# Expert blocks of an MoE layer on one core: another order of the weight loads, another interleaving of large and small experts, and a shorter gather for the first small expert

## The chip, the cores and the metric

The kernel runs on one core of a Trainium2 chip. The metric is the device time of one execution in microseconds (us). A core has several engines with their own instruction streams, each worked off strictly in order: PE (TensorE, matrix products), DVE (VectorE), ACT (ScalarE), POOL (GpSimd) and SP (SyncE), which here issues nearly all transfers from memory (HBM) into the on-chip memory (SBUF). Results of PE land in PSUM, of which the other engines read them. An instruction that needs something of another engine waits for a semaphore, and everything behind it on its own engine waits too.

## The reference, cut to what matters

Two transformer blocks on 256 tokens of width 1024. Everything ahead of the last stage is left as it is; the change lies in the last stage, a mixture of eight experts, with two experts for each token:

```
def moe_swiglu(x, router_w, w_gate, w_up, w_down):
    logits = (x @ router_w).astype(jnp.float32)
    top_v, top_i = lax.top_k(logits, TOP_K)
    gates = jax.nn.softmax(top_v, axis=-1)
    combine = jnp.sum(jax.nn.one_hot(top_i, N_EXPERTS, dtype=jnp.float32) * gates[..., None], axis=-2)
    y = jnp.zeros_like(x)
    for e in range(N_EXPERTS):
        y = y + combine[..., e:e + 1].astype(x.dtype) * swiglu(x, w_gate[e], w_up[e], w_down[e])
    return y
```

`swiglu` is `(silu(x @ w_gate) * (x @ w_up)) @ w_down`, with 3584 hidden columns for each expert, all in float32. The three matrices of an expert are 44 MB, those of all eight 352 MB (336 loads of 1 MB), and each is read once.

## The kernel before

**Experts and blocks.** The experts are sorted by how many tokens they have and put into eight places, in turn a large and a small one. A place has a fixed number of token slots (`SLOTS`): 128 for the large ones (even places, called many here), 64, 64, 64 and 32 for the small ones (odd places, called few). The hidden columns of an expert are taken in 7 blocks of 512, so that there are 28 many blocks, m0 to m27, and 28 few blocks, f0 to f27. A block takes 6 loads of 1 MB: two halves each of gate, up and down.

**A many block.** Each half of weights goes through `weights`: a 1 MB load into a raw buffer, a rounded copy `whi` by ACT (L437, CAST), and the rest, weight minus `whi`, by DVE (L438), both for products in a faster number format, with three products for each tile: token-hi by weight-hi, token-lo by weight-hi, token-hi by weight-lo. `proj` does gate, then up; `act` makes silu(gate) times up (ACT L1919, DVE L1920); `turn` transposes it on PE into the PSUM tile `t`, from which ACT takes the rounded copy `mh` (L1940 CAST) and DVE the rest (L1940); `down` multiplies with the down weights, into the PSUM tiles `s`. Where a few block follows, the down weights of a many block are loaded and split ahead of that block's products and kept in `WD`.

**A few block.** The weights are multiplied straight from the raw buffers, in float32, without ACT and DVE (`passing`, `proj_few`). Gate and up stand side by side in one PSUM tile `mm`; after both halves `act` copies it to SBUF by ACT (`msg<-mm`, L1917 COPY), and `turn` transposes it and makes the product (L1934, L1935).

**The order.** The program is written block by block, and each engine gets its instructions in an order that follows from the code order and from priorities (`ahead` moves a piece forward). Inside block n stand: the first half of its products, `turn` of block n-1, the second half, `act`, then `down` of block n-1. So PE does the down products of a many block right behind the second half of the few block that follows it. The order of the blocks follows from `BEHIND`, by how many blocks the few ones lag: m0 m1 m2 f0 m3 f1 m4 f2 ... m27 f25 f26 f27.

**Buffers.** The raw buffers (called `room`, `raw`, and by the names of dead tiles: `x`, `xlo`, `oht`, `my`) are handed out in a ring in the order of the calls. SP issues a load only when its buffer has been read by its last user, and the loads behind it on SP wait as well.

**Gather.** `gather(q)` collects the tokens of place q and of place q+1 by products with a 0/1 matrix `oh`, from the hi and the lo part of the tokens apart. For the first few expert it is called a second time with `some=False`: 32 products of 256 columns, of which only the 64 slots of place 1 are taken over, by 8 DVE instructions (L1805, L1806).

Of the kernel before, what the change touches and what calls it, by code (L numbers as in the profile page):

```python
# [11 lines left out]
F32 = mybir.dt.float32  # L12
# [10 lines left out]
KC = 8  # L23
# [10 lines left out]
RANKS = (None, 3, 0, 4, 1, 5, 2, 6)  # L34
SLOTS = (128, 64, 128, 64, 128, 64, 128, 32)

BEHIND = 2.5, 2.5

SPLITS = (("dsa_q", 256), ("dsa_k", 64), ("dsa_v", 64), ("idx_q", 256), ("idx_k", 32), ("idx_w", 8),
          ("fox_q", 384), ("fox_k", 384), ("fox_v", 384), ("fox_f", 6), ("nsa_q", 384), ("nsa_kc", 128),  # L40
# [243 lines left out]
class Net:  # L284
# [1410 lines left out]
    def _moe(self, x, out):  # L1695
        nc, d, hw, tc = self.nc, self.d, self.hw, self.tc
        y = self.xp.tile([128, 2, D], F32, name="y", tag="xhi")
# [4 lines left out]
        oh = own("oh").rearrange("p (b e s) -> p b e s", b=2, e=NE)  # L1702
        rt = self.router.rearrange("p (k e) -> p k e", k=KC)
        bf = self.c["before"].rearrange("p (a b) -> p a b", a=8)
        at = self.psum("t")
        hold, kept = self.hold, []
        for tb in range(2):
            ts = slice(tb * 128, tb * 128 + 128)
            with self.ahead(5000):

                p = self.psum("o")
                for k in range(KC):
                    r = nc.tensor.matmul(p[:, 0:8], x[:, k, ts], rt[:, k], start=k == 0, stop=k == KC - 1)
                q = lg[:, tb]
# [17 lines left out]
                b = nc.vector.tensor_scalar(oh[:, tb, 0], self.c["iota"], slot[:, tb, 0:1], None, op0=ALU.is_equal)  # L1732

                for c in range(2):
                    p = self.psum("s" if tb else "mm")
# [4 lines left out]
                    i = self.split(xh[:, tb, cs], xl[:, tb, cs], p)  # L1740
                    if tb:
                        self.after(i, b)
                        b = i
# [19 lines left out]
        def back(oh, dt):  # L1763

            ohf = oh.bitcast(F32) if dt is F32R else oh
            oht = self.late.tile([128, NE, T], dt, name="oht", tag="oht")
            for e in range(0, NE, 2):
                p = self.psum()
                for i in range(2):
                    for tb in range(2):  # L1770
                        t = self.tr(p[:, i * 256 + tb * 128:i * 256 + tb * 128 + 128], ohf[:, tb, e + i], self.ident)
                        self.after(t, gm)
                i = nc.scalar.copy(oht[:, e:e + 2], p.rearrange("p (e t) -> p e t", e=2))
                self.after(i, gx)
            return oht

        own_g = own("g")
        gh, gl = (own_g[:, i * 1024:i * 1024 + 1024].rearrange("p (k s) -> p k s", k=KC) for i in range(2))

        FX = {}  # L1780

        def gather(q, tags="mm", low=nc.vector.tensor_copy, some=True, few=True):

            if few:
                w = SLOTS[q + 1]
                fx = FX[q + 1] = hw.tile([128, KC, 64], F32, name="fx", tag="fx", bufs=2)
            for k in range(0, KC, 2):
                for src, dst, ev, tag in ((xh, gh, nc.scalar.copy, tags), (xl, gl, low, tags)):
                    p = self.psum(tag)
                    for i in range(2):  # L1790
                        for tb in range(2):
                            o = oh[:, tb, q:q + 2] if few else oh[:, tb, q][:, None].to_broadcast([128, 2, 128])
                            last = self.mm(p[:, i * 256:i * 256 + 256], src[:, tb, (k + i) * 128:(k + i) * 128 + 128], o,
                                           start=tb == 0, stop=tb == 1)
                    p = p.rearrange("p (k s) -> p k s", k=2)
                    if src is xh:
                        ph = p
                        if some:
                            a = ev(gh[:, k:k + 2], p[:, :, 0:128])
                    else:  # L1800
                        if some:
                            b = ev(gl[:, k:k + 2], p[:, :, 0:128])
                        if few:
                            fxk = fx[:, k:k + 2, 0:w]
                            nc.vector.tensor_copy(fxk, ph[:, :, 128:128 + w])  # L1805
                            nc.vector.tensor_tensor(fxk, fxk, p[:, :, 128:128 + w], op=ALU.add)  # L1806
                yield
            if some:
                if low == nc.scalar.copy:
                    a, b = b, None  # L1810
                self.hold = a, b or self.hold[1], None
                kept[:] = a, b, last

        b1 = b
        early = [[(None, i0)] * 3 + [(None, b)], (None, b)]
        late, kept = kept, [None] * 3
        with self.ahead(5000):
            for _ in gather(0, low=nc.scalar.copy, few=False):
                pass
# [16 lines left out]
        p = self.psum("o")[:, 0:8]  # L1836
        for tb in range(2):
            nc.tensor.matmul(p, self.ones, sel[:, tb], start=tb == 0, stop=tb == 1)
        i = nc.vector.tensor_copy(cnt, p)
# [32 lines left out]
        def block_of(n, q, b, hf):  # L1872

            if q == 0:
                return d[n][0, b, hf]
            return d[n][bass.ds(expert[q], 1), b, hf].rearrange("e p n -> (e p) n")

        H, YD, PP, WD = {}, {}, {}, {}

        def proj(e, b, n, steps=iter(())):  # L1880

# [17 lines left out]
        def proj_few(e, b, hf):  # L1899

            p = PP[e, b] = PP.pop((e, b)) if hf else self.psum()
            with self.ahead(3000):
                ws = [self.passing(block_of(n, e, b, hf)) for n in ("mgate", "mup")]
            m = SLOTS[e]
            n = 8 * m
            for i in range(4):
                k = hf * 4 + i
                for r in range(0, 128, m):
                    w, c = ws[r // 64], r % 64 // m * n
                    self.mm(p[r:r + m, 0:n], FX[e][:, k, 0:m], w[:, i * 512 + c:i * 512 + c + n], start=k == 0,  # L1910
                            stop=k == KC - 1, tile_position=(0, r), skip_group_check=True)
# [101 lines left out]

        mh = None
        many, few = ([(e, b) for e in range(i, NE, 2) for b in range(7)] for i in range(2))
        at = {f: i + np.interp(i, (0, len(few) - 1), BEHIND) for i, f in enumerate(few)}
        at.update((m, i) for i, m in enumerate(many))
        blocks = sorted(at, key=at.get)
        first = blocks.index(few[0])
# [1 line left out]
        for n, (e, b) in enumerate(blocks):  # L2021
            if n == 2:
                for q in range(1, NE):
                    expert[q] = nc.values_load(idi[0:1, q:q + 1], engines=(mybir.EngineType.SP,), min_val=1, max_val=NE - 1)
            if n == 9:

                mc = hw.tile([128, 1], F32, name="mc")
                over = hw.tile([128, 8], F32, name="over")

                nc.vector.memset(cap[:, 0:1], 128.0)  # L2030
                nc.vector.tensor_scalar(cap[:, 1:8], rank[:, 1:8], 2.5, 64.0, op0=ALU.is_lt, op1=ALU.mult)
                nc.vector.tensor_scalar(over[:, 1:8], rank[:, 1:8], 5.5, 32.0, op0=ALU.is_lt, op1=ALU.mult)
                nc.vector.tensor_tensor(cap[:, 1:8], cap[:, 1:8], over[:, 1:8], op=ALU.add)
                nc.vector.tensor_scalar(cap[:, 1:8], cap[:, 1:8], 32.0, None, op0=ALU.add)
                nc.vector.tensor_tensor(over, cnt, cap, op=ALU.subtract)
                nc.vector.tensor_reduce(mc, over, axis=AX.X, op=ALU.max)
                nc.vector.tensor_scalar(mc, mc, 0.0, None, op0=ALU.max)
                mci = hw.tile([128, 1], I32, name="mci")
                nc.vector.tensor_copy(mci, mc)
            if n == 7:  # L2040
                oht = back(oh, F32R)
            steps = iter(())
            if e % 2 and blocks[n - 1][0] % 2 == 0:
                WD[blocks[n - 1]] = [self.weights(block_of("mdown", *blocks[n - 1], hf)) for hf in range(2)]
            if e % 2:
                proj_few(e, b, 0)
            else:
                proj(e, b, "mgate")
            if n == 1:
                mh = hw.tile([128, 2, 2, 512], F32R, name="mh", tag="mh")  # L2050
            if n:
                turn(*blocks[n - 1])
            if n + 1 == first:
                steps = gather(0, some=False)
            if e % 2:
                proj_few(e, b, 1)
            else:
                if b == 6 and e + 2 < NE:
                    steps = gather(e + 2)
                proj(e, b, "mup", steps)  # L2060
            act(e, b)
            if n < 2:

                i = by_place(qcomb, comb) if n else places(oh, qslot, range(1, NE), True)
                self.hold = self.hold[0], i, None
            if n:
                down(*blocks[n - 1], steps)
            for _ in steps:
                pass
            if n > 2 and blocks[n - 2][1] == 6:  # L2070
                scatter(blocks[n - 2][0])
            if n == len(blocks) - 5:
                gb = self.rows()
# [12 lines left out]
        with tc.If(most > 0):  # L2086
# [3 lines left out]
            oh = own("oh", F32).rearrange("p (b e s) -> p b e s", b=2, e=NE)  # L2090
# [127 lines left out]
```

## Time and profile before

| | before |
|---|---|
| time of a run, median of 3 | 1853.82 us (1853.0 to 1855.28) |
| time of the profiled execution | 1856.29 us |
| its span in the profile | 1854.5 us |
| PE busy | 1783.7 us (96%) |
| DVE busy | 1073.1 us (58%) |
| ACT busy | 867.3 us (47%) |
| read from HBM | 493.81 MB |

Busy time is the time in which at least one instruction of an engine runs. The expert blocks take the last part of the span, from about 990 us on.

### The profile page before, as it was taken

The page shows a single profiled execution, that of the slowest core. Times are in us where ns is not written, and L with a number is a line of the kernel's source. Part 1 is how long each engine was busy: PE and PEld are TensorE (multiplying, and loading weights), DVE is VectorE, ACT ScalarE, POOL GpSimd, SP SyncE. Part 2 cuts the span into 40 slices and gives each one's busy share as a digit, 9 for nine tenths or more (in the row PEclk, how much of TensorE's full clock was granted, in tenths as well). Part 3 has the DMA queues.
Part 4 walks back from the last instruction along what each step waited for, and adds up shares of the span by engine and source line. Part 5 has one row for each costly group of instructions (what it writes and reads, how often), then busy time and mean ns, then how long its engine had stood idle before and what let it go on. Part 6 is the DMA issues. An engine that isn't in the chain of part 4 may idle for free. (4 is left out here: it accounts for less than half of the span.)

```text
span 1854.5 us, 27561 instructions
## 1 busy us (share of the span) xinstructions
PE 1783.7 (96%) x11038; PEld 1351.6 (73%) x11038; DVE 1073.1 (58%) x1586; ACT 867.3 (47%) x1291; POOL 33.3 (2%) x78
## 2 busy tenths in 40 slices
PE   7999999999999999999999999999999999999984
PEld 5777788778896999888977766665656566665652
DVE  3765688757644754466437755565556565565543
ACT  3454375545553544345345545444535444444531
POOL 1000010000000000000010000000000000000000
PEclk9999999999999999989998999999999999999997
DMA  9654443234211555543028799999999999999996
GB/s 386 257 225 167 175 160 125 69 115 171 92 54 63 196 184 172 197 146 117 24 102 338 287 398 394 411 413 420 421 421 421 421 421 421 421 421 420 421 420 250
DMA packets 71175, 497.71 MB, mean 268 GB/s; under 512 B 8226, under 2 KB 9538, under 8 KB 11264
## 3 DMA queue, kind: packets, MB, share of 16 engines
q1 hardware_dynamic: 70752, 495.39, 67.8%
q8 instruction: 89, 1.46, 0.3%
q0 software_dynamic: 288, 0.48, 0.1%
q14 instruction: 46, 0.38, 0.1%
HBM read 493.81 MB, written 1.05 MB: 267 GB/s over the span
## 5 line engine op out<-in xcount | busy, mean ns | idle before, releaser
L438 DVE TENSOR_TENSOR raw<-raw,whi 128x2048 fp32r<-128x2048 f32 (+1 forms) x157 | 279.8, 1800 | 198.9 <-ACT whi L437 198.2
L437 ACT CAST whi<-raw 128x2048 fp32r<-128x2048 f32 (+1 forms) x198 | 306.6, 1570 | 160.7 <-PE mm L459 48.6
L413 PE MATMUL mm<-whi,g 128*128 128x512 f32 x896 | 227.3, 396 | 2.5 <-DVE y L2011 2.5
L413 PEld LDWEIGHTS mm<-whi,g 128*128 128x128 f32 x896 | 166.4, 189 | 38.9 <-issue 4.5
L437 ACT CAST whi<-room 128x2048 fp32r<-128x2048 f32 (+1 forms) x97 | 172.9, 1803 | 31.7 <-PE mm L413 13.5
L458 PE MATMUL mm<-xhi,whi 128*128 128x256 f32 x720 | 182.1, 288 | 0.7 <-ACT whi L437 0.7
L459 PE MATMUL mm<-xlo,whi 128*128 128x256 f32 x720 | 180.4, 286 | 0.0
L413 PE MATMUL mm<-room,fx 128*64 128x512 f32 (+1 forms) x632 | 152.1, 526 | 10.6 <-DMA room<-in_mup_dram 7.2
L458 PEld LDWEIGHTS mm<-xhi,whi 128*128 128x128 f32 x720 | 137.7, 191 | 8.1 <-issue 5.6
L459 PEld LDWEIGHTS mm<-xlo,whi 128*128 128x128 f32 x720 | 137.7, 191 | 1.5 <-issue 1.4
L438 DVE TENSOR_TENSOR room<-room,whi 128x2048 fp32r<-128x2048 f32 x47 | 107.6, 2289 | 31.7 <-ACT whi L437 29.7
L413 PE MATMUL s<-whi,mh 128*128 128x512 f32 x448 | 117.2, 404 | 0.0
L413 PEld LDWEIGHTS s<-whi,mh 128*128 128x128 f32 x448 | 82.6, 189 | 37.9 <-issue 19.9
L463 PE MATMUL mm<-xhi,raw 128*128 128x256 f32 x720 | 104.3, 285 | 0.0
L413 PE MATMUL mm<-raw,fx 128*64 128x512 f32 (+1 forms) x344 | 91.5, 508 | 6.5 <-DMA raw<-in_mup_dram 6.5
L1940 ACT CAST mh<-t 128x512 fp32r<-128x512 f32 x28 | 16.4, 585 | 169.5 <-PE t L416 169.4
L463 PEld LDWEIGHTS mm<-xhi,raw 128*128 128x128 f32 x720 | 93.6, 191 | 1.2 <-DVE cin L1219 0.9
L413 PEld LDWEIGHTS mm<-room,fx 128*64 128x64 f32 (+1 forms) x632 | 47.9, 129 | 57.4 <-issue 38.9
L438 DVE TENSOR_TENSOR raw<-room,whi 128x2048 fp32r<-128x2048 f32 x30 | 68.7, 2291 | 32.7 <-ACT whi L437 31.5
L438 DVE TENSOR_TENSOR room<-raw,whi 128x2048 fp32r<-128x2048 f32 x30 | 68.8, 2292 | 28.4 <-ACT whi L437 26.9
L1920 DVE TENSOR_TENSOR msg<-msg,mm 128x512 f32<-128x512 f32 x28 | 19.3, 688 | 100.5 <-PE mm L413 100.5
L413 PEld LDWEIGHTS mm<-raw,fx 128*64 128x64 f32 (+1 forms) x344 | 28.0, 125 | 47.6 <-issue 35.6
(590 smaller groups left out, 3264.3 us busy)
## 6 DMA issues: line engine op xcount, KB each, us to landing
room<-in_mup_dram SPq DMA_DIRECT2D x66, 1024.0 KB, 13.0
room<-in_mdown_dram SPq DMA_DIRECT2D x60, 1024.0 KB, 18.0
room<-in_mgate_dram SPq DMA_DIRECT2D x55, 1024.0 KB, 15.2
raw<-in_mdown_dram SPq DMA_DIRECT2D x41, 1024.0 KB, 17.1
raw<-in_mgate_dram SPq DMA_DIRECT2D x38, 1024.0 KB, 12.8
raw<-in_mup_dram SPq DMA_DIRECT2D x33, 1024.0 KB, 18.8
raw<-in_win_dram SPq DMA_DIRECT2D x29, 1024.0 KB, 6.4
raw<-in_din_dram SPq DMA_DIRECT2D x24, 1024.0 KB, 4.8
```

The source lines that it names most:

```text
L413: return self.kept(self.nc.tensor.matmul(*a, **k))
L437: a = nc.scalar.copy(h[:, v], r[:, v])
L438: b = nc.vector.tensor_tensor(lo[:, v], r[:, v], h[:, v].bitcast(F32), op=ALU.subtract)
L458: nc.tensor.matmul(out, w, xh[:, k], start=start and i == 0, stop=False)
L459: nc.tensor.matmul(out, w, xl[:, k], start=False, stop=False)
L463: nc.tensor.matmul(out, lo[:, off + i * 128:off + i * 128 + 128], xh[:, k], start=False, stop=stop and i == n - 1)
L1920: self.after(nc.vector.tensor_tensor(sg, sg, PP.pop((e, b, "mup")), op=ALU.mult), self.parted[1])
L1940: i = nc.scalar.copy(hh, pt), nc.vector.tensor_tensor(hl, pt, hh.bitcast(F32), op=ALU.subtract)
```

## The change

Three things. First, the lag of the few blocks is given by a table: it falls from 2.5 to 0.6 over the first seven few blocks, stays there until the 21st and rises to 2.5 again at the last. The blocks stand then as m0 m1 m2 f0 m3 f1 f2 m4 f3 m5 f4 f5 m6 f6 m7 f7 ... m21 f21 m22 m23 f22 m24 f23 m25 f24 m26 f25 m27 f26 f27. Second, a few block's four gate and up loads are called before the down weights of the many block ahead of it, and kept in `GU`; before, those down weights were called first. Third, the tokens of the first few expert are gathered by 32 products of 64 columns in float32, straight from `y`, into one PSUM tile, with one DVE copy.

```diff
-BEHIND = 2.5, 2.5
+BEHIND = (0, 6, 20, 27), (2.5, 0.6, 0.6, 2.5)
...
-        def gather(q, tags="mm", low=nc.vector.tensor_copy, some=True, few=True):
+        def gather(q, tags="mm", low=nc.vector.tensor_copy, few=True):
...
+        def gather_few():
+
+            fx = FX[1] = hw.tile([128, KC, 64], F32, name="fx", tag="fx", bufs=2)
+            p = self.psum()
+            for k in range(KC):
+                for tb in range(2):
+                    self.mm(p[:, k * 64:k * 64 + 64], y[:, tb, k * 128:k * 128 + 128], oh[:, tb, 1, 0:64].bitcast(F32),
+                            start=tb == 0, stop=tb == 1)
+                if k % 2:
+                    yield
+            nc.vector.tensor_copy(fx, p.rearrange("p (k s) -> p k s", k=KC))
...
         def proj_few(e, b, hf):
 
             p = PP[e, b] = PP.pop((e, b)) if hf else self.psum()
-            with self.ahead(3000):
-                ws = [self.passing(block_of(n, e, b, hf)) for n in ("mgate", "mup")]
+            ws = GU.pop((e, b, hf))
...
-        at = {f: i + np.interp(i, (0, len(few) - 1), BEHIND) for i, f in enumerate(few)}
+        at = {f: i + np.interp(i, *BEHIND) for i, f in enumerate(few)}
...
+            if e % 2:
+
+                with self.ahead(3000):
+                    for hf in range(2):
+                        GU[e, b, hf] = [self.passing(block_of(w, e, b, hf)) for w in ("mgate", "mup")]
             if e % 2 and blocks[n - 1][0] % 2 == 0:
                 WD[blocks[n - 1]] = [self.weights(block_of("mdown", *blocks[n - 1], hf)) for hf in range(2)]
...
             if n + 1 == first:
-                steps = gather(0, some=False)
+                steps = gather_few()
```

What stands where on the engines is shown for the block f1 and the down products of m3 ahead of it; the other pairs look alike. First ACT before the change: the two casts of m3's down weights (out of `room_10451` and `raw_10457`), the cast of `mh` (m3's), and then the copy of f1's projections out of PSUM, which waits for PE (as every L1917).

```order
L437 CAST whi<-room_10399 128x2048 [waits DMAHW0_49,DVE_49,PE_49]
L437 CAST whi<-room_10417 128x2048 [waits DMAHW1_49,DVE_49,PE_49]
L1934 ACTIVATE msg<-t 128x256 [waits PE_49]
L1919 ACTIVATE msg<-mm 128x512
L437 CAST whi<-room_10451 128x2048 [waits DMAHW4_49,DVE_49]
L437 CAST whi<-raw_10457 128x2048 [waits DMAHW5_49,DVE_49,PE_49]
L1940 CAST mh<-t 128x512 [waits PE_49]
L1917 COPY msg<-mm 128x512 [waits DVE_49,PE_49]
```

ACT at the same place with the change (the copy is L1925 now, the cast of `mh` L1948, and m3's down weights lie in `x` and `raw_10435`):

```order
L437 CAST whi<-room_10369 128x2048 [waits DMAHW0_49,DVE_49,PE_49]
L437 CAST whi<-room_10387 128x2048 [waits DMAHW1_49,DVE_49,PE_49]
L1927 ACTIVATE msg<-mm 128x512 [waits PE_49]
L1942 ACTIVATE msg<-t 128x256 [waits PE_49]
L1925 COPY msg<-mm 128x512 [waits DVE_49,PE_49]
L437 CAST whi<-x 128x2048 [waits DMAHW0_49]
L437 CAST whi<-raw_10435 128x2048 [waits DMAHW1_49]
L1948 CAST mh<-t 128x512
```

The copy of f1 has moved from behind the two casts and `mh` to ahead of all three.

PE at that place with the change: the last products of f1's second half, and then m3's down products (`s`), the first of which waits for ACT and the second for DVE. This order is the same before.

```order
L413 MATMUL mm<-room_10425,fx 64x512
L413 MATMUL mm<-xlo,fx 64x512
L413 MATMUL s<-whi,mh 128x512 [waits Activation_49]
L413 MATMUL s<-whi,mh 128x512 [waits DVE_49]
L413 MATMUL s<-whi,mh 128x512 x6
L413 MATMUL s<-room_10432,mh 128x512 x4
```

Between f1's products and m3's down products PE has nothing else, so that the second group starts only when ACT and DVE have `mh` and the down weights ready.

DVE there, with the change: the lo parts of m3's two down halves and then of `mh`, each of which waits for ACT.

```order
L1943 TENSOR_TENSOR msg<-msg,t 128x256 [waits Activation_49]
L1928 TENSOR_TENSOR msg<-msg,mm 128x512 [waits PE_49]
L438 TENSOR_TENSOR room_10432<-x,whi 128x2048 [waits DMAHW0_49,DVE_49,Activation_49]
L438 TENSOR_TENSOR x<-raw_10435,whi 128x2048 [waits DMAHW1_49,DVE_49,Activation_49]
L1948 TENSOR_TENSOR mh<-t,mh 128x512 [waits PE_49,Activation_49]
```

This piece of DVE has not moved against its neighbours; what it waits for on ACT has.

SP's loads before: f0's down halves, m3's down halves, and then f1's gate and up.

```order
L385 DMA raw_10445<-in_mdown_dram 128x2048 [waits DMAHW3_49,DVE_49,PE_49]
L385 DMA room_10451<-in_mdown_dram 128x2048 [waits DMAHW4_49,DVE_49,PE_49]
L385 DMA raw_10457<-in_mdown_dram 128x2048 [waits DMAHW5_49,DVE_49,PE_49]
L385 ISA
L385 DMA room_10464<-in_mgate_dram 128x2048 [waits DVE_49,DMAHW6_49,PE_49,Activation_49]
...
L385 DMA x<-in_mup_dram 128x2048 [waits DMAHW1_49,DVE_49,PE_49]
```

SP's loads with the change:

```order
L385 DMA raw_10415<-in_mdown_dram 128x2048 [waits DMAHW3_49,DVE_49,PE_49]
L385 ISA
L385 DMA room_10421<-in_mgate_dram 128x2048 [waits DMAHW4_49,DVE_49,PE_49]
...
L385 DMA xlo<-in_mup_dram 128x2048 [waits DMAHW7_49,DVE_49,PE_49]
L385 DMA x<-in_mdown_dram 128x2048 [waits DMAHW0_49,PE_49]
L385 DMA raw_10435<-in_mdown_dram 128x2048 [waits DMAHW1_49,PE_49]
```

f1's four loads now stand ahead of m3's two.

## Rows read from the trace of the kernel before

**Rows 1.** Waits of PE, 1006 to 1680 us: total, times, longest.

```profile
PE mm L413 <- DVE y L2011: 2.0, 2, 1.0
```

**Rows 2.** Windows: PE, PEld, DVE, ACT, POOL busy (instructions), PEclk, DMA share, GB/s.

```profile
1045.00:1055.00 10.00, 10.00 (x56) 8.50 (x54) 8.62 (x12) 3.82 (x2) 0.00 (x0) 1.00 0.65 222
1055.00:1070.00 15.00, 15.00 (x68) 8.29 (x67) 5.13 (x3) 6.70 (x5) 0.00 (x0) 1.00 0.51 190
1200.00:1680.00 480.00, 477.95 (x2205) 295.92 (x2204) 273.35 (x197) 215.61 (x175) 0.00 (x0) 1.00 1.01 420
```

**Rows 3.** Timeline of PE, one pair: start, duration, operation, count.

```profile
1090.82 0.59 PE L413 MATMUL mm<-x,fx 128*64 128x512 f32 x1
1091.35 2.13 PE L413 MATMUL s<-whi,mh 128*128 128x512 f32 x8
```

**Rows 4.** Timeline of ACT, same pair; in brackets the idle time before and its releaser.

```profile
1087.87 0.59 ACT L1940 CAST mh<-t 128x512 fp32r<-128x512 f32 x1 [8.63 <-PE t L416]
1091.46 0.59 ACT L1917 COPY msg<-mm 128x512 f32<-128x512 f32 x1 [3.01 <-PE mm L413]
1091.95 1.91 ACT L437 CAST whi<-raw 128x2048 fp32r<-128x2048 f32 x1
```

**Rows 5.** Timeline of DVE: `mh` and lo parts of an early pair, lo parts of the pair above.

```profile
1026.30 0.68 DVE L1940 TENSOR_TENSOR mh<-t,mh 128x512 fp32r<-128x512 f32 x1
1026.90 2.28 DVE L438 TENSOR_TENSOR room<-room,whi 128x2048 fp32r<-128x2048 f32 x1
1029.10 0.68 DVE L1920 TENSOR_TENSOR msg<-msg,mm 128x512 f32<-128x512 f32 x1
...
1093.89 2.29 DVE L438 TENSOR_TENSOR raw<-raw,whi 128x2048 fp32r<-128x2048 f32 x1 [4.71 <-ACT whi L437]
1096.27 2.29 DVE L438 TENSOR_TENSOR raw<-room,whi 128x2048 fp32r<-128x2048 f32 x1
```

**Rows 6.** Waits of PE from 1680 to 1854 us (as rows 1).

```profile
PE mm L413 <- DMA room<-in_mup_dram: 7.2, 5, 1.9
PE mm L413 <- DMA raw<-in_mup_dram: 6.5, 4, 2.0
PE mm L413 <- SPq L2086: 3.1, 2, 2.6
PE o L413 <- SPq L2086: 2.9, 3, 1.3
PE o L413 <- DMA room<-in_mdown_dram: 1.3, 1, 1.3
```

**Rows 7.** Windows of low granted clock (columns as in rows 2).

```profile
1711.00:1714.50 3.50, 3.37 (x28) 1.36 (x28) 0.00 (x0) 0.00 (x0) 0.00 (x0) 0.52 1.01 417
...
1827.20:1830.60 3.40, 3.40 (x36) 1.73 (x40) 0.00 (x0) 0.00 (x0) 0.00 (x0) 0.50 0.96 400
990.90:1004.60 13.70, 12.18 (x57) 12.05 (x58) 8.91 (x31) 5.39 (x12) 0.38 (x1) 0.50 1.01 421
```

**Rows 8.** Timeline of PE in and after two of them.

```profile
1782.54 3.55 PE L413 MATMUL mm<-whi,g 128*128 128x512 f32 x8
...
1786.98 1.98 PE L413 MATMUL mm<-whi,g 128*128 128x512 f32 x8
...
1827.11 3.15 PE L413 MATMUL mm<-room,fx 128*32 128x256 f32 x26 [2.59 <-SPq L2086]
```

**Rows 9.** Timeline of PE: a fourth of the second gather.

```profile
1042.90 0.64 PE L413 MATMUL mm<-oh,xth 128*128 128x256 f32 x4
1043.38 0.64 PE L413 MATMUL mm<-oh,xtl 128*128 128x256 f32 x4
```

**Rows 10.** Groups of PE's instructions: count, busy, mean ns, idle before.

```profile
L1515 PE MATMUL mm<-Y,XT 128*128 128x64 f32 x160 | 19.7, 270 | 0.0
```

**Rows 11.** Timeline of SP: start, issue time, load.

```profile
1055.28 0.34 SPq L385 DMA_DIRECT2D xlo<-in_mup_dram  x1
1066.04 0.33 SPq L385 DMA_DIRECT2D oht<-in_mgate_dram  x1
```

More of the change, by code (lines that the diff above doesn't have):

```diff
@@ L1797, in gather @@
                         ph = p
-                        if some:
-                            a = ev(gh[:, k:k + 2], p[:, :, 0:128])
-                    else:
-                        if some:
-                            b = ev(gl[:, k:k + 2], p[:, :, 0:128])
+                        a = ev(gh[:, k:k + 2], p[:, :, 0:128])
+                    else:
+                        b = ev(gl[:, k:k + 2], p[:, :, 0:128])
                         if few:
@@ L1807, in gather @@
                 yield
[L1808 to L1812, printed above, removed]
+            if low == nc.scalar.copy:
+                a, b = b, None
+            self.hold = a, b or self.hold[1], None
+            kept[:] = a, b, last
+        def gather_few():
[8 more added lines that the diff above has]
+            nc.vector.tensor_copy(fx, p.rearrange("p (k s) -> p k s", k=KC))
         b1 = b
@@ L1876, in block_of @@
             return d[n][bass.ds(expert[q], 1), b, hf].rearrange("e p n -> (e p) n")
-        H, YD, PP, WD = {}, {}, {}, {}
+        H, YD, PP, WD, GU = {}, {}, {}, {}, {}
         def proj(e, b, n, steps=iter(())):
```

## The prediction

> **What bounds the kernel now.** I went first to the windows of the expert blocks. From 1200 to 1680 us the transfer engines are fully busy (share 1.01, 420 GB/s) and PE is busy for 477.95 of 480 us at full granted clock [rows 2]. So two engines are at their limit at once there, and the average over the span (PE 96%) doesn't tell which of them a delay would hit. The list of PE's waits does: between 1006 and 1680 us PE waited 2.0 us in all, in two waits [rows 1]. A pair of a many and a few block takes 12 loads, 12 x 1.0486 MB / 0.420 = 30.0 us, so these 674 us are about 22 pairs, and PE has 0.1 us of slack in each. Whatever makes PE stand still for longer in a pair lengthens the kernel, whether or not the loads could go faster. Only after 1680 us does PE wait for loads: 21.0 us, the sum of the five largest lines [rows 6].
>
> Then I followed one pair over the three engines. PE ends the few block's products at 1090.82 + 0.59 = 1091.41 and begins the many block's down products (`s<-whi,mh`) at 1091.35, the ends being modelled: no gap [rows 3]. On ACT `mh` is made at 1087.87, while PE is still in the few block's second half, and the last thing ACT does for the pair is the copy of the few block's products, at 1091.46, after 3.01 us of waiting for PE [rows 4]. Nobody waits for that copy soon: its transposes stand behind the next products. ACT is idle for 8.63 us ahead of `mh` and DVE for 4.71 us ahead of its next lo part [rows 4, 5]; that idleness costs nothing.
>
> **The copy moves ahead of the casts.** The order shows what the change does to this pair: called after the few block's four loads, the splits of the down weights rank behind the few block's copy. ACT now has copy, cast, cast, `mh`. The copy waits for the end of the few block's products, call it T0. PE's next instructions are the down products, which wait for `mh` and for the lo part of `mh`; those stand on ACT and DVE behind the two casts and two lo parts that now can't begin before T0. This is a wait in a ring of work: PE waits for ACT, which had waited for PE.
>
> Its price, step by step from the rows: the copy starts at T0 + 0.05 (1091.41 to 1091.46), the first cast 0.49 later (1091.46 to 1091.95) [rows 4]; the lo part of it 1.94 after that (1091.95 to 1093.89); the second lo part 2.38 later (1093.89 to 1096.27); the lo part of `mh` 2.20 later, the distance of a lo part to the next thing on DVE (1026.90 to 1029.10); done 0.60 later (1026.30 to 1026.90) [rows 5]. The sum is T0 + 7.66. The second cast and `mh` on ACT lie beside this (T0 + 0.54 + 1.8 + 1.8 + 0.5 = T0 + 4.6). PE can do 1 of the pair's 24 down products meanwhile, 2.13 / 8, about 0.25 [rows 3]. So PE stands still for 7.4 us in such a pair.
>
> How often: there are 28 copies. Four have no down products of a many block behind them (f0, where the order still has the casts ahead; f2 and f5, which follow a few block; f27 at the end). Of the other 24, 22 have both casts behind the copy, and two (at m13 and m20) one cast ahead and one behind. For these the chain is 0.05 + 0.49 + 1.94 + 2.20 + 0.60 - 0.25 = 5.0. Together 22 x 7.4 + 2 x 5.0 = **172.8 us**. If DVE's distances were at the short end throughout, or semaphores took longer, this would shift by 0.5 us a pair, 12 in all.
>
> **What it gives back.** With 7.4 us more, a pair takes PE over 37 us against 30.0 us of loads, so that PE alone is the bound and loads run ahead until the buffers are full. The waits for loads after 1680 us go: **-21.0** [rows 6]. In that part PE's granted clock fell to half four times for 3.4 us, after it had waited for loads [rows 7]; a product that takes 1.98 for eight took 3.55 there [rows 8]. That goes with the waits: 4 x 1.7 = **-6.8**. Both belong to the pairs' own time; the stalls above are added to what is left.
>
> **What the stalls do to the clock.** A PE that stood still comes back at half clock: after 2.59 us without work, 1827.20 to 1830.60 ran at 0.50 [rows 7, 8]; the stretches last 3.4 us, and one early, amid scattered short waits, 13.7 us. No row shows a stop of 7.4 us in full work. Bounds: nothing (the stretch falls into the stop), and 3.4 us for each (two stretches in work at half speed). I take the row, one stretch: 24 x 1.7 = **+40.8**. The Trainium skill bears on this term: "TensorE: Matmul & The Clock Gate", section "HAM oscillation", tells of a kernel with 32 stops of 3 to 5 us that lost 26.7 us to the low clock, which is 0.83 us for each. By the page the term would be 24 x 0.83 = 20 and the total some 21 us lower; the rows of this kernel, whose stretches lie wholly in work, say 1.7, and I keep to them.
>
> **The loads in the order of reading, and the lag.** Four loads of the few block now go ahead of two of the many block, and SP waits for other buffers. Before 1070 us loads were lost: SP held the next one back from 1055.28 to 1066.04 [rows 11], and the share was 0.65 over 10 us and 0.51 over 15 us, 3.5 + 7.4 = 10.9 us of transfer time [rows 2]. Under a PE that needs 37 us for a pair this is worth nothing; it is the first rival's gain. **The gather:** 32 products of 0.12 (0.48 for four, 1042.90 to 1043.38) [rows 9] go, and 32 of 128x64 in float32 come, nearest row 19.7 / 160 = 0.123 each [rows 10]: 3.8 against 3.9, +0.1. At double that price it would be 4 us. Seven DVE instructions go, beside PE work.
>
> **Sum** on the span: 1854.5 - 21.0 - 6.8 + 172.8 + 40.8 + 0.1 = 2040.4. The median of the runs, 1853.82, is 0.7 below that span (the profiled run itself, 1856.29, 1.8 above). So **2040 us**, 10% slower.
>
> **Rivals.**
> *Faster: the loads are the bound and the stalls hide behind them.* For it speaks the share of 1.01 in [rows 2], and the Trainium skill beside it ("Perfetto Trace Analysis", section "Roofline") gives about 120% of 358 GB/s, some 430, as a single core's practical ceiling, which 420 is near: by that rule only transfers would count. Then the order of ACT costs nothing and the 10.9 us of lost transfers come back at the end, where PE waits 21.0 us for them: 1843 at best; with some of it kept, as the new order also waits for buffers, 1846. The point that decides is the slack of PE in a pair. It would have to be above 7.4 us and is 0.1 [rows 1]. It could win only if ACT in fact reached the casts earlier than the order says. 6%.
> *Heavier clock.* The half clock lasts 13.7 us after each stop, as at 990.9 [rows 7]: 6.8 in place of 1.7, 24 x 5.1 = 122 more, 2162. Against it: all later stretches were 3.4 us. 5%.
> *No clock loss.* The stop swallows the low stretch, PE comes back at full clock: 2040 - 41 = 1999. 8%.
> *The stalls are there but a second thing covers them* (the gain of the loads and a shorter chain balance): only with a stall below 0.6 us. 2%.
>
> **How the numbers follow.** My forecast has 79%, with its own range of 1999 to 2081 (clock term 0 to 82). The range takes the no-clock case and the 12 us of the chain in on both sides: 1985 to 2090; outside are the faster case, the balance, the heavier clock, together 13%, and some tails. A measurement of this kernel tells 0.2% (3.7 us) from no change. Slower by more: 79 + 5 + 8 = 92%; faster: 6%; same: 2%.
>
> **What would show it.** Right: PE waits of about 7 us in nearly every pair, at `s<-whi,mh`, released by DVE's `mh`, some 170 us in all; ACT with the copy first and casts close behind; DMA share well under 1 from 1200 us on; no wait of PE for loads at the end; granted clock at half right after the stops. Wrong: PE waits of under 1 us there, which would mean that casts ran ahead of the copy; or a DMA share that stays at 1.01 beside a span near 1845.

## The result, and the profile after

The changed kernel takes **2048.44 us** (median of 4 runs, 2044.97 to 2051.01); the kernel before, on the same chip, 1854.55 us. The ratio is 1.1044, 95% interval 1.1024 to 1.1064. Its profiled execution has a span of 2046.3 us, 191.8 more than before.

From the page of the changed kernel, busy time of the first engine and the slices of 51 us (tenths):

```profile
span 2046.3 us, 27689 instructions
PE 1833.5 (90%) x11038; PEld 1387.0 (68%) x11038; DVE 1070.3 (52%) x1579; ACT 865.2 (42%) x1291; POOL 33.3 (2%) x78
PEclk9999999999999999999898998889898899889887
DMA  9655442342125554302798998788888889889893
```

DVE and ACT are busy for as long as before, PE for 50 us longer with the same number of products, and the kernel is 192 us longer: nobody has more work. From slice 22 on the granted clock is below full in most slices, and the transfer share in most of them in the 0.8s, where before it was full (1.01 in [rows 2]). The windows (columns as in [rows 2]) say the same of the steady part:

```profile
1055.00:1070.00 15.00, 15.00 (x68) 9.13 (x65) 6.79 (x5) 7.78 (x6) 0.00 (x0) 1.00 0.95 356
1200.00:1680.00 480.00, 396.33 (x1665) 245.28 (x1662) 209.51 (x157) 168.06 (x138) 0.00 (x0) 0.89 0.86 325
```

Against [rows 2], PE is busy for 396 of 480 us in place of 478, the transfers move 325 GB/s in place of 420, and the hole in the transfers at 1055 us is nearly gone (0.95 in place of 0.51). The waits of PE, from 990 us to the end:

```profile
PE s L413 <- ACT mh L1948: 110.3, 24, 4.8
PE s L413 <- DVE mh L1948: 54.1, 24, 2.5
PE mm L413 <- DVE y L2019: 1.4, 3, 0.5
PE o L413 <- DVE msg L1943: 0.7, 1, 0.7
```

There are 24 stops, each in two parts, all at the first two down products of a many block (`s`), and together they make 164.4 us. No wait for a load is left: the lines of [rows 6] have no counterpart. One stop, on PE, then ACT, then DVE, in the timeline of the changed kernel:

```profile
1089.04 0.59 PE L413 MATMUL mm<-xlo,fx 128*64 128x512 f32 x1
1094.42 0.80 PE L413 MATMUL s<-whi,mh 128*128 128x512 f32 x1 [4.79 <-ACT mh L1948]
1097.45 3.35 PE L413 MATMUL s<-whi,mh 128*128 128x512 f32 x7 [2.23 <-DVE mh L1948]
```

```profile
1089.70 0.59 ACT L1925 COPY msg<-mm 128x512 f32<-128x512 f32 x1 [16.28 <-PE mm L413]
1090.18 1.90 ACT L437 CAST whi<-x 128x2048 fp32r<-128x2048 f32 x1
1091.98 1.90 ACT L437 CAST whi<-raw 128x2048 fp32r<-128x2048 f32 x1
1093.78 0.59 ACT L1948 CAST mh<-t 128x512 fp32r<-128x512 f32 x1
```

```profile
1092.12 2.29 DVE L438 TENSOR_TENSOR room<-x,whi 128x2048 fp32r<-128x2048 f32 x1 [12.95 <-ACT whi L437]
1094.50 2.29 DVE L438 TENSOR_TENSOR x<-raw,whi 128x2048 fp32r<-128x2048 f32 x1
1096.71 0.68 DVE L1948 TENSOR_TENSOR mh<-t,mh 128x512 fp32r<-128x512 f32 x1
```

This is how to read the three together. PE's last product of the few block ends at 1089.04 + 0.59 = 1089.63. Up to there ACT stood idle, for 16.28 us until its copy began, and DVE for 12.95 us until its first lo part, because the copy at the head of ACT's queue waited for PE ([rows 4] shows the copy last and nothing waiting behind it). Then the chain runs off while PE waits: copy, cast, lo, lo, `mh`'s lo, to 1097.45.

The granted clock in and after two of these stops (windows; 0.50 is 1.2 of 2.4 GHz):

```profile
1092.40:1102.70 10.30, 6.05 (x13) 4.42 (x14) 4.90 (x3) 1.97 (x2) 0.00 (x0) 0.50 0.61 256
1147.00:1153.90 6.90, 4.37 (x11) 3.48 (x11) 4.68 (x3) 2.23 (x2) 0.00 (x0) 0.51 0.56 235
```

The low stretches begin within the stop, last 6.8 or 10.2 us as a rule, and cover some 4 to 7 us of work, the first product and what follows the stop taken together. The eight products that took 2.13 in [rows 3] take 0.80 and 3.35 = 4.15 us here, with 2.23 us of waiting between the first and the other seven.

### The profile page after: what moved, and what is told of

Its sections match the earlier page's. It is cut to its first block, busy times and chain, and to the rows that moved or that the text cites. A ratio compares the mean times of both kernels' runs of the same rounds, so it can differ in the third digit from the quotient of the medians.

```text
span 2046.3 us, 27689 instructions
## 1 busy us (share of the span) xinstructions
PE 1833.5 (90%) x11038; PEld 1387.0 (68%) x11038; DVE 1070.3 (52%) x1579; ACT 865.2 (42%) x1291; POOL 33.3 (2%) x78
## 5 line engine op out<-in xcount | busy, mean ns | idle before, releaser
L438 DVE TENSOR_TENSOR raw<-raw,whi 128x2048 fp32r<-128x2048 f32 (+1 forms) x170 | 309.5, 1837 | 260.2 <-ACT whi L437 259.7
L437 ACT CAST whi<-raw 128x2048 fp32r<-128x2048 f32 (+1 forms) x202 | 313.7, 1575 | 202.6 <-PE s L413 58.7
L413 PE MATMUL s<-whi,mh 128*128 128x512 f32 x448 | 166.5, 518 | 164.4 <-ACT mh L1948 110.3
L413 PEld LDWEIGHTS s<-whi,mh 128*128 128x128 f32 x448 | 110.6, 254 | 220.0 <-ACT mh L1948 129.0
L437 ACT CAST whi<-room 128x2048 fp32r<-128x2048 f32 (+1 forms) x93 | 165.3, 1796 | 88.0 <-PE s L413 73.0
L1925 ACT COPY msg<-mm 128x512 f32<-128x512 f32 (+1 forms) x28 | 14.9, 533 | 312.2 <-PE mm L413 312.2
L438 DVE TENSOR_TENSOR room<-raw,whi 128x2048 fp32r<-128x2048 f32 x27 | 61.8, 2291 | 89.3 <-ACT whi L437 89.2
L438 DVE TENSOR_TENSOR room<-room,whi 128x2048 fp32r<-128x2048 f32 x37 | 84.7, 2289 | 20.2 <-ACT whi L437 19.1
L413 PE MATMUL mm<-raw,fx 128*64 128x512 f32 (+1 forms) x280 | 85.5, 560 | 0.0
L438 DVE TENSOR_TENSOR xlo<-room,whi 128x2048 fp32r<-128x2048 f32 x11 | 25.2, 2292 | 83.5 <-ACT whi L437 83.5
```

Source lines behind the costliest of these rows:

```text
L413: return self.kept(self.nc.tensor.matmul(*a, **k))
L437: a = nc.scalar.copy(h[:, v], r[:, v])
L438: b = nc.vector.tensor_tensor(lo[:, v], r[:, v], h[:, v].bitcast(F32), op=ALU.subtract)
L1925: nc.scalar.copy(sg[:, 0:n], PP.pop((e, b))[:, 0:n])
```

## The experiments

All kernels were compared with runs of the kernel before on the same chip, in three groups.

**The copy back behind the casts.** Is it the place of that one instruction? In the changed kernel one dependency is added, which holds the few block's copy behind the cast of `mh`; then ACT has cast, cast, `mh`, copy in every pair.

```diff
-                nc.scalar.copy(sg[:, 0:n], PP.pop((e, b))[:, 0:n])
+                self.after(nc.scalar.copy(sg[:, 0:n], PP.pop((e, b))[:, 0:n]), turned.pop() if turned else None)
...
                 for a, p in zip(i, self.parted):
                     self.after(a, p)
+                turned.append(i[0])
...
```

> The changed kernel with one dependency more: the copy of the few block's products is put behind the cast of mh on ACT, so that ACT has cast, cast, mh, copy again. Theory A (the place of the copy alone makes the stops): PE's waits at the down products go from 164 us to under 5, the granted clock goes back to 1.0 from 1010 us on, and the time is that of before less what the new load order gives, 1843 to 1855 us. Rival B (the down weights are loaded too late now and the casts wait for them): waits of several us in each pair stay, now released by DMA, 1950 us or more. Rival C (the shorter lag leaves the pairs too close together): the waits stay, 2000 us or more.

Measured: 1848.96 us, ratio 0.9969 (0.9956 to 0.9981). Its waits of PE from 1006 us on, and the steady windows:

```profile
PE s L413 <- DVE mh L1948: 10.0, 5, 2.5
PE s L413 <- ACT mh L1948: 9.1, 4, 3.4
```

```profile
1200.00:1680.00 480.00, 474.49 (x2232) 300.20 (x2228) 279.38 (x204) 223.84 (x182) 0.00 (x0) 1.00 1.01 421
```

In this stretch the stops, the low clock and the idle transfers are gone, with the loads in the new order, the new lag and the new gather all in place. ACT at f1 in the repaired kernel:

```profile
1072.22 1.91 ACT L437 CAST whi<-x 128x2048 fp32r<-128x2048 f32 x1
1074.02 1.92 ACT L437 CAST whi<-raw 128x2048 fp32r<-128x2048 f32 x1
1084.99 0.58 ACT L1948 CAST mh<-t 128x512 fp32r<-128x512 f32 x1 [9.06 <-PE t L416]
1088.62 0.59 ACT L1925 COPY msg<-mm 128x512 f32<-128x512 f32 x1 [3.04 <-PE mm L413]
```

So m3's raw down weights were there at 1072 us, while in the changed kernel the first of the same two casts began at 1090.18. Nothing else differs: in the two traces the loads of SP, the products of PE and the instructions of DVE follow each other in the same order (by operation and tile name), and on ACT 24 copies stand elsewhere and no other instruction. Theories B and C fall.

Two points of the expectation missed. Of waits at `mh` 19.1 us stayed, not under 5: one stop of 3.0 us at 1646 us, the others after 1700 us; and the clock fell again behind those (0.53 from 1718.5 to 1725.2 us). There the loads are late as they were before [rows 6], and in the new order the late ones are the down weights, which come last and still have to be cast and split. ACT's timeline of the repaired kernel, at such a place:

```profile
1713.24 1.90 ACT L437 CAST whi<-x 128x2048 fp32r<-128x2048 f32 x1 [9.65 <-DMA x<-in_mdown_dram]
1715.46 1.90 ACT L437 CAST whi<-room 128x2048 fp32r<-128x2048 f32 x1 [0.33 <-DMA room<-in_mdown_dram]
1717.27 0.58 ACT L1948 CAST mh<-t 128x512 fp32r<-128x512 f32 x1
```

So rival B's mechanism exists, in the last 130 us. These 16 us of waits stand where the kernel before had the 21.0 us of [rows 6], with the transfer engines busy (share 1.01 from 1700 to 1820 us in both), so they probably cost nothing more; no run tests it.

**Each part alone.** The order of the loads alone, on the kernel before (the hunks `GU` of the change and no other):

```diff
-            with self.ahead(3000):
-                ws = [self.passing(block_of(n, e, b, hf)) for n in ("mgate", "mup")]
+            ws = GU.pop((e, b, hf))
...
+            if e % 2:
+
+                with self.ahead(3000):
+                    for hf in range(2):
+                        GU[e, b, hf] = [self.passing(block_of(w, e, b, hf)) for w in ("mgate", "mup")]
```

> The kernel before with the order of the loads alone (gate and up of a few block called ahead of the down weights), old lag, old gather. In its ACT order the copy stands ahead of both casts in 21 pairs and ahead of one in 4. Theory A: 21 x 7 + 4 x 5 = 167 us of waits and some 55 us of low clock, less 28 us at the end: about 2045 us. Rival C (the lag does it): within 10 us of before.

Measured: 2055.39 us, ratio 1.1086 (1.1067 to 1.1105), with these waits:

```profile
PE s L413 <- ACT mh L1939: 111.8, 25, 4.8
PE s L413 <- DVE mh L1939: 55.8, 25, 2.5
```

25 stops, 167.6 us (167 expected). The time is 10 us above the 2045 expected, in part because the low clock costs more than the 55 put in for it: the span is 2053.0, and 2053.0 - 1854.5 = 167.6 - 23.0 (the waits of [rows 1, 6]) - 6.8 + 60.7, which is 2.4 for each stop. So the order of the loads alone brings the whole loss, and the scheduler's answer to it, the copy ahead of the casts, is the way by which it does, as the run further on with this order and the copy held behind `mh` shows.

The lag table alone:

```diff
-BEHIND = 2.5, 2.5
+BEHIND = (0, 6, 20, 27), (2.5, 0.6, 0.6, 2.5)
...
```

> The kernel before with the lag table alone. The copy stays behind the casts in the ACT order. Theory A: no stops at the down products, 1845 to 1862 us. Rival C: stops of several us in each pair, 2000 us or more.

Measured: 1853.85 us, ratio 0.9992 (0.9983 to 1.0001). At the down products PE waits once, for 2.3 us, where the changed kernel has 24 stops.

The shorter gather alone:

```diff
-                steps = gather(0, some=False)
+                steps = gather_few()
...
```

> The kernel before with the shorter float32 gather alone. By the rows 32 products of 0.12 us are replaced by 32 of about the same time, and seven DVE instructions go beside PE work: within 1.5 us of before (1852 to 1856). If a 64-column float32 product took double, 4 us more at that place, of which the waits for loads at the end may take back all.

Measured: 1854.38 us, ratio 1.000 (0.9991 to 1.0009). The group of its products in the changed kernel shows the price:

```profile
L413 PE MATMUL mm<-oh,y 128*128 128x64 f32 x32 | 4.0, 268 | 0.0
```

4.0 / 32 = 0.125 us each, against 0.123 in [rows 10].

**The copy on another engine.** If the fault is that work which is ready stands behind work that waits, it isn't tied to ACT. Here the changed kernel makes the copy on DVE, without a dependency.

```diff
-                nc.scalar.copy(sg[:, 0:n], PP.pop((e, b))[:, 0:n])
+                nc.vector.tensor_copy(sg[:, 0:n], PP.pop((e, b))[:, 0:n])
```

> The changed kernel with the copy on DVE in place of ACT, no dependency added. In the order it stands on DVE ahead of the two lo parts of the down weights, while ACT makes its casts and mh early. Theory A, for any engine that is read in order: PE stops again, but for the shorter chain copy, lo, lo, mh's lo: 0.05 + 0.5 + 2.4 + 2.2 + 0.6 - 0.25 = 5.5 us a pair, released by DVE alone, about 130 us in all, 2000 to 2025 us with the low clock. If ACT itself were what is short (its casts too slow), taking the copy off it would bring the time back to about 1850.

Measured: 2007.28 us, ratio 1.0819 (1.0796 to 1.0842). A stop of it, on PE and on DVE, and PE's waits:

```profile
1097.10 0.49 PE L413 MATMUL s<-whi,mh 128*128 128x512 f32 x1
1103.17 3.35 PE L413 MATMUL s<-whi,mh 128*128 128x512 f32 x7 [5.58 <-DVE mh L1948]
```

```profile
1097.24 0.69 DVE L1925 COPY msg<-mm 128x512 f32<-128x512 f32 x1 [10.54 <-PE mm L413]
1097.85 2.28 DVE L438 TENSOR_TENSOR room<-x,whi 128x2048 fp32r<-128x2048 f32 x1
1100.22 2.29 DVE L438 TENSOR_TENSOR x<-raw,whi 128x2048 fp32r<-128x2048 f32 x1
1102.43 0.68 DVE L1948 TENSOR_TENSOR mh<-t,mh 128x512 fp32r<-128x512 f32 x1
```

```profile
PE s L413 <- DVE mh L1948: 130.2, 25, 5.6
```

The first down product now goes at once, since ACT made its casts early; the second waits 5.58 us for DVE (5.5 expected), 130 us in all. There are 25 stops, one more than before, as f0's copy now has a lo part behind it too. The stop follows the queue in which the copy stands.

**What the low clock costs.** In the changed kernel PE does 28 products more in each of the 25 pairs, f0's included; they serve nothing and fill the time in which PE would stand still.

```diff
+            if e % 2 and blocks[n - 1] in WD:
+                p = self.psum()
+                for i in range(28):
+                    self.mm(p, gh[:, 0], gh[:, 0:4].rearrange("p k s -> p (k s)"), start=True, stop=True)
             if n:
                 down(*blocks[n - 1], steps)
```

> The changed kernel with 28 products of 128x512 more in each such pair, into a PSUM tile that nobody reads, between the few block's products and the down products: work of about 6.3 us that PE does while it would stand still. It adds no useful work; f0's pair, where there was no stop, gets longer by 6.3, the two pairs of 5 us by 1.5. If the low clock costs what the difference of the traces says (191.8 us longer, of which 142.4 are waits, so 49 more than before, 56 in all), the clock stays at full and the time falls by 56 - 9 = about 47, to about 2000 us. If the low clock cost nothing, the time rises by 9 or more, to 2057.

Measured: 2008.97 us, ratio 1.0828 (1.0806 to 1.085): 39 us less than the changed kernel (40 by the two ratios, as the two ran in different groups), with 700 products more. One of the pairs in its timeline, and its waits:

```profile
1147.79 6.64 PE L413 MATMUL mm<-g 128*128 128x512 f32 x28
1154.27 0.40 PE L413 MATMUL s<-whi,mh 128*128 128x512 f32 x1
1155.69 1.90 PE L413 MATMUL s<-whi,mh 128*128 128x512 f32 x7 [1.02 <-DVE mh L1948]
```

```profile
PE s L413 <- DVE mh L1948: 21.2, 22, 1.0
```

The seven products take 1.90 in place of 3.35, and the granted clock's mean over the span is 0.987 (0.939 with the stops). The spans give the price: 2046.3 - 2008.2 = 38.1 less, although 25 x 6.48 = 162.0 of work came (1147.79 to 1154.27) and only 164.4 - 21.2 = 143.2 of waits went. So the low clock costs 38.1 + 162.0 - 143.2 = **56.9 us**, 2.4 for each stop. This is the difference of one execution of each kernel, and those of the changed kernel lie 6 us apart, so a few us are open. The time fell by 39 and not by the 47 expected: the products took 6.48 in place of 6.3, and a wait of 1.0 stayed behind most of them, so that filling cost 162.0 - 143.2 = 18.8 in place of 9.

**Where the repaired kernel's gain is from, and whether there is more.** The order of the loads with the copy held behind `mh`, but with the old lag and the old gather:

```diff
+            ws = GU.pop((e, b, hf))
...
+                self.after(nc.scalar.copy(sg[:, 0:n], PP.pop((e, b))[:, 0:n]), turned.pop() if turned else None)
...
```

> The new order of the loads on the kernel before (old lag, old gather), with the copy held behind the cast of mh. The lag table alone gave a ratio of 0.9992 and the gather alone 1.000, so if the gain of the repaired kernel (0.9969) is that of the loads' order, this one shows it too: 0.995 to 0.998, 1846 to 1852 us, with the transfers some 10 us ahead of before at 1230 us. If it needs the lag and the order together, this one is within 0.1% of before.

Measured: 1848.71 us, ratio 0.9962 (0.9947 to 0.9977). Within the noise the whole gain of the repaired kernel is that of the loads' order.

The repaired kernel with the first few block's loads behind the down weights again:

```diff
+            if e % 2 and blocks[n - 1][0] % 2 == 0 and n == first:
+                WD[blocks[n - 1]] = [self.weights(block_of("mdown", *blocks[n - 1], hf)) for hf in range(2)]
             if e % 2:
...
-            if e % 2 and blocks[n - 1][0] % 2 == 0:
+            if e % 2 and blocks[n - 1][0] % 2 == 0 and n > first:
```

> The changed kernel with the copy held behind mh, and the first few block alone with its gate and up loads behind the down weights again. In the repaired kernel SP stood still from 992.92 to 1009.21 before the first load of a chosen expert, and the transfer share was 0.66 from 990 to 1005 us (1.00 before the change), 5 us of transfer time. With two loads of m2 ahead of that wait again, the loads go on. If the transfers set the end, up to 5 us less than the repaired kernel: 1842 to 1849 us. If the buffers of the loads behind give the time back, the same as the repaired kernel within 1.5 us.

Measured: 1852.01 us, ratio 0.9982 (0.9973 to 0.9991). Neither expectation fits: it is 3 us above the repaired kernel, though the intervals of the two ratios overlap. Two of its windows:

```profile
990.00:1005.00 15.00, 11.83 (x55) 11.62 (x56) 10.15 (x35) 5.71 (x13) 0.87 (x1) 0.57 1.01 419
...
1055.00:1070.00 15.00, 15.00 (x67) 8.12 (x67) 5.05 (x4) 5.97 (x5) 0.00 (x0) 1.00 0.46 171
```

The early hole is closed (share 1.01), and the old one is back 60 us later (0.46): SP issues no load from 1056.19 to 1066.94 us, and the next one goes into `oht`, as in [rows 11]. So the buffers that are filled early are probably not free later; what held that load is open.

The repaired kernel with a lag that falls within two few blocks:

```diff
-BEHIND = (0, 6, 20, 27), (2.5, 0.6, 0.6, 2.5)
+BEHIND = (0, 2, 20, 27), (2.5, 0.6, 0.6, 2.5)
```

> The repaired kernel (copy held behind mh) with the lag falling to 0.6 within two few blocks in place of six: m0 m1 m2 f0 f1 f2 m3 f3 m4 ... From 990 to 1070 us before lost about 20 us of transfer time and the repaired kernel about 14, since PE frees the buffers more slowly than they could be filled; a few block takes PE 11 us for the same six loads for which a many block takes 17. If that is what the repaired kernel still loses, buffers come free sooner here and the time falls by up to 5 us more: 1843 to 1848 us. If the wait for the chosen experts (SP stands still to 1009 us) and the chain after it set the loss, no change: 1847 to 1851.

Measured: 1845.24 us, ratio 0.9946 (0.9932 to 0.9959), the lowest ratio here. One window from 990 to 1250 us, of the kernel before, of the repaired one and of this one:

```profile
990.00:1250.00 260.00, 257.96 (x1200) 175.77 (x1201) 163.03 (x179) 132.05 (x116) 0.87 (x1) 0.97 0.92 370
```

```profile
990.00:1250.00 260.00, 258.62 (x1208) 169.85 (x1207) 152.24 (x167) 125.33 (x115) 0.00 (x0) 0.98 0.95 383
```

```profile
990.00:1250.00 260.00, 258.62 (x1208) 169.90 (x1208) 151.52 (x165) 126.79 (x115) 0.00 (x0) 0.98 0.95 387
```

260 us at 370, 383 and 387 GB/s are 96.2, 99.6 and 100.6 MB; at 420 GB/s the lead is 8 and 10.5 us, and the medians are 6.7 and 10.6 us below the kernel before. The same window of the order of the loads with the copy held (old lag, old gather), and of the run with the first few block's loads late:

```profile
990.00:1250.00 260.00, 257.57 (x1197) 175.31 (x1198) 162.95 (x180) 131.84 (x116) 0.87 (x1) 0.97 0.94 382
990.00:1250.00 260.00, 255.71 (x1193) 167.56 (x1194) 153.66 (x174) 123.70 (x114) 0.87 (x1) 0.97 0.94 380
```

Their leads are 7.4 and 6.2 us, and their medians 7.1 and 3.8 below. So in three of these four kernels what is moved earlier in that stretch is saved at the end, and in one only part of it. Against the repaired kernel and against the loads' order with the copy held, which ran in other groups, the intervals of this ratio overlap, so that this last step is likely and not certain.

## Why the prediction was right, step by step

**The bound.** That PE had no slack (2.0 us in 674) and not the transfers decided held: with the stops the transfers fell to a share of 0.86 and PE never waited for them.

**The copy's place.** Right in mechanism and in count: 24 stops, 22 long ones and two of one cast, all at the instructions named. Right in size within 5%: 164.4 us against 172.8. The chain itself was 7.82 us (1089.63 to 1097.45) where I had 7.66; what I mis-sized is the one product that PE does meanwhile. The 0.25 is the distance of products in a row; one by itself takes 0.49 even at full clock (1097.10, with the copy on DVE), and in this stop, at half clock, 0.80, so that 7.02 were left as waiting. The two short stops were 3.0 + 1.94 = 4.9, forecast 5.0. That the place of the copy is the cause, and not late weights or the lag, is shown by the repaired kernel, in which only the copies stand elsewhere, and by the loads alone. One reading was loose: f0 does have down products behind it (m2's); it has no stop because its casts stay ahead.

**What it gives back.** All waits for loads went, and with them the low clock that followed them, as forecast. Of the 21.0 us that I summed as waits for loads, 6.0 stand against SP at a branch (L2086) and not against a load [rows 6]; they went too, and what released them is open.

**The low clock.** This term was too small: 40.8 forecast, 56.9 measured by keeping PE busy. The difference of the profiles gives about the same: 191.8 = 164.4 - 23.0 (the waits of [rows 1, 6]) - 6.8 + 57.2. I had taken one stretch of 3.4 us per stop, from stops of 2 to 2.6 us [rows 7, 8]; after a stop of 7 us the stretch was two or three times as long, of which 4 to 7 us lay in work. The measured 2.4 a stop is inside the bounds (0 to 3.4). The Trainium skill's page "TensorE: Matmul & The Clock Gate", section "HAM oscillation", has 26.7 us for 32 stops, 0.83 each, in another kernel, whose stops are shorter. These runs show nearly three times that, and the measurement decides.

The two errors, 8 too much and 16 too little, partly cancel; 2040 against 2048 is closer than the terms are, and that part of it is luck. The range was also put together loosely: 1999 - 12 and 2081 + 12 are 1987 and 2093, not 1985 and 2090.

**The gather and the lag.** 0.125 us a product, forecast 0.123; neither part alone moves the time measurably.

**The rivals.** The faster one named a real gain that was hidden: once the stops were repaired, the loads' order was worth 0.3 to 0.4%, 6 to 7 us of the 10.9 that I had bounded it by, and 1849 us against the 1846 given for it. What decided against it was PE's slack, as its point of decision said. "No clock loss" and "heavier clock" both fell: 57 us lies between 0 and 163.

Why the scheduler ranks the copy ahead once the loads are called in the other order was not tested; that it did so, and that one dependency undoes it, is what the runs show.

## What to carry to other kernels

When loads are called in another order, compare the order on the engines that are *not* the bound, too: an instruction that waits for the bottleneck must not stand ahead of work on which the bottleneck waits next, or the idle time of the other engines turns into a stop. Price such a ring as the whole chain behind the waiting instruction, times the number of places, and add what the clock loses after each stop. And a loss of this kind can hide a gain: look for the part of the change that was good, and tie down the order with a dependency before throwing it away.

## What the runs showed of the hardware that was not expected

After a stop of 5 to 7 us the granted clock was at half (1.2 GHz) for mostly 6.8 or 10.2 us, longer than the 3.4 us seen after shorter stops; 4 to 7 us of that were paid in work, which cost 2.4 us a stop. Filling the stops with 6.5 us of useless products made the kernel 39 us faster (2048.44 to 2008.97): PE then stayed at full clock (granted 1.00 from 1200 to 1680 us, where it was 0.89).
